# Moving the modulation blocks of a two-layer PEER block into its first expert search, with fewer expert columns ahead

## The chip, the cores and the metric

One core of one Trainium2 chip runs the whole program. The metric is device microseconds (us) for one execution. Engines are called TensorE (PE in the profile; PEld is its weight load), VectorE (DVE), ScalarE (ACT), GpSimd (POOL) and SyncE (SP, the queue from which nearly all transfers are issued, in order).

## The reference, cut to what matters

512 tokens of width 1024 pass through two blocks. Each has a token mixer (gated linear attention in the first, retention and stick-breaking attention in the second) and then PEER, a feed-forward layer with 16384 single-neuron experts: eight heads pick 16 experts each per token by product keys.

```python
def peer(h, w_query, sub_keys, expert_down, expert_up):
    ...
    top_s, top_i = lax.top_k(sub_scores, K)
    ...
    best_s, best_c = lax.top_k(cand_s.reshape(T, PEER_HEADS, K * K), K)
    ...
        act = jax.nn.gelu(a, approximate=False) * gb
        v = expert_up[ib]
        return jnp.einsum('pe,ped->pd', act.astype(xb.dtype), v)
```

The second block is modulated: `mod = silu(c) @ ada_w + ada_b` gives six rows of 1024 values, which scale, shift and gate the second block. They depend on `c` alone, so they can be made at any time before the second block starts.

## The kernel before, in words

A float32 product is made of three matmuls (high times high, low times high, high times low), for which every weight is split: ScalarE copies it to a high part (`uH`, `VH`, `WH`), VectorE subtracts that from the original (`uL`, `VL`, `WL`).

Each of the two PEER layers runs in two parts, one after the other on the same engines.

*The search.* `top_k` makes the query product (`qy`), the key scores (`sc`) and VectorE's top 16 of them, in 16 steps. Then `pick` combines candidates, and for three of the four token tiles a one-hot product writes a dense table of gates to DRAM: 32 steps per tile, each with two comparisons on VectorE (`oh`, `og`, L1022 and L1025) and eight small matmuls (`pg`, L1042). Into all this the search weaves matmuls of the dense product of tokens with the experts' inputs, `pu` (L908, class `Inward`), as filler: `PICK_MM` per step of `pick`, `QUAD_MM` per step of the first two tiles, `LAST_MM` per step of the third. 24 of these matmuls make the activations of 128 experts, `A`; two such columns are a group, and there are 64 groups. `NEARLY` of them are made ahead in the search, and their `A` goes to DRAM (`ad`, L981). The cap on the filler is `NEARLY * 48 + 144`.

*The loop.* It runs over the 64 groups p. Each takes 36 matmuls of 512 columns into `acc` (L119 to L121), for which VectorE makes `W = A * G` (L1102), two `WL` and two `VL` (L1088). Groups not made ahead are made here: where group p+2 is such a group, 48 `pu` matmuls are woven into p. `load_a(p + LA)` at the start of p loads the `A` that went to DRAM; `A` has 12 buffers. The first token tile's experts are not dense: their rows are gathered by GpSimd's indirect transfers (L864) into `gr` and used by VectorE as dot products (L876) and sums (L883). The fetches not made in the search (190 of 256) are spread over the loop by a weight per group, 4 for a group with `pu` matmuls and 1 for one without, up to the sixth group from the end.

*The modulation.* 48 blocks of 128 outputs are each a transfer of 512 KB (`aw`) and a row-wise product with `silu(c)`, summed. 22 are made before the first mixer. The other 26 were split: `side(step, pool)`, called once per step of the first `top_k` (steps -16 to -1) and once per second group of the first loop (steps 0 to 16), took one block per step. In the search GpSimd multiplies (L1689) and ScalarE sums (L1685); in the loop VectorE does both in one instruction (L1177). Step 15 adds the bias, step 16 writes the result to DRAM and reads two rows back.

*The seams.* Between the layers, small row-wise operations stand alone: `hg = h * gf` (L1736, GpSimd for three of four tiles), `h + sh` (L1745, GpSimd for one), `xn + shift` (L199, GpSimd for three), `h + m` (L1797, GpSimd for half), and the last additions (L1833, GpSimd for three halves). The other instances run on VectorE.

Of the kernel before, what the change touches and what calls it, by code (L numbers as in the profile page):

```python
# [17 lines left out]
ALU = mybir.AluOpType  # L18
# [5 lines left out]
NT = 4  # L24
# [8 lines left out]
JUMPS = (16, 8, 5, 4, 3, 2, 2, 2)  # L33
SUBE = lambda nc: nc.vector
GRP = 2
NEARLY = 44
NHELD = 0
FRONT = 4
MLAG = 1
# [9 lines left out]
MT = 16  # L49
FW = 4  # L50
WB = (0, 2)
LA = 2
AB = FRONT + 2
HGP = (0, 1, 2)
ADA = (8, 7, 7)
ADA0 = 0
SHB = (0,)
HALVES = ((0, 512), (512, 1024))
S1 = 2
YR = 2  # L60
# [14 lines left out]
M2_LAG = 4  # L75
SB = 1
SPE = 0
SHP = 3
RP_ACT = (0, 1)
PICK_MM = 40  # L80
QUAD_MM = 20
LAST_MM = 16
PK = 2
LAG = 3
DOT = (2, 2, 1)
# [7 lines left out]
class K:  # L93
# [83 lines left out]
    def rms_rows(self, pool, t, row, gain, out=None, shift=None, known=None):  # L177

        nc = self.nc
        rs = pool.tile([128, 1], F32, name=f"rs{t}", tag="rrs", bufs=NT)
        j = pool.tile([128, D], F32, name="rsj", tag="rsj", bufs=1)
        o = 512 if known is not None else 0
        self.square_mean(rs, j[:, o:], row[:, o:])
        yield
        if known is None:
            nc.vector.tensor_scalar(rs, rs, EPS, None, op0=ALU.add)
        else:
            nc.vector.scalar_tensor_tensor(rs, rs, EPS, known, op0=ALU.add, op1=ALU.add)  # L190
        nc.gpsimd.tensor_tensor(rs, rs, self.mhalf, op=ALU.pow)
        if out is None:
            out = pool.tile([128, D], F32, name=f"xn{t}", tag="xn", bufs=NT)
        yield
        for c in HALVES:
            c = slice(*c)
            nc.vector.scalar_tensor_tensor(out[:, c], row[:, c], rs, gain[:, c], op0=ALU.mult, op1=ALU.mult)
            if shift is not None:
                (nc.gpsimd if t < SHP else nc.vector).tensor_tensor(out[:, c], out[:, c], shift[:, c], op=ALU.add)  # L199
        yield  # L200
        self.turn(out, t)

# [972 lines left out]
def ada_block(K_, b, raw, cs, mod):  # L1175

    K_.nc.vector.scalar_tensor_tensor(raw, raw, 1.0, cs, op0=ALU.mult, op1=ALU.mult, accum_out=mod[:, b:b + 1])  # L1177
# [363 lines left out]
def body(tc, a, out, stop=None):  # L1541
    nc = tc.nc
    with ExitStack() as ctx:
        k = K(ctx, tc, a)
        c = k.const
# [5 lines left out]
        mod = c.tile([128, 48], F32, name="mod")  # L1551
# [127 lines left out]
        def side(step, pool):  # L1679

            if step == -15:
                nc.scalar.activation(cs, cs, AF.Silu)
            while summing:
                b, raw = summing.pop(0)
                nc.scalar.activation(raw, raw, AF.Copy, accum_out=mod[:, b:b + 1])  # L1685
            while loaded:
                b, raw = loaded.pop(0)
                if step < 0:
                    nc.gpsimd.tensor_tensor(raw, raw, cs, op=ALU.mult)  # L1689
                    summing.append((b, raw))  # L1690
                else:
                    ada_block(k, b, raw, cs, mod)
            if left and step >= -15 and step != -2 and step != -1:
                raw = wide(pool, 6) if step < 0 else wide(pool)
                nc.sync.dma_start(raw, a["ada_w"][left[0]])
                loaded.append((left.pop(0), raw))
            if step == MT - 1:
                nc.vector.tensor_tensor(mod, mod, ab, op=ALU.add)
                for i in range(2):
                    s = mod[:, 24 * i + 8:24 * i + 16]  # L1700
                    nc.vector.tensor_scalar(s, s, 1.0, None, op0=ALU.add)
                    nc.vector.tensor_tensor(s, s, ng[:, i], op=ALU.mult)
            if step == MT:
                p = k.mm_tile("mt", tag="u")
                nc.tensor.transpose(p[:48, :128], mod, k.ident)
                m = wide(pool)
                nc.scalar.activation(m[:48, :128], p[:48, :128], AF.Copy)
                nc.sync.dma_start(modd, m[:48, :128])
                row(cs, 1)
                sh.append(row(wide(pool), 0))  # L1710

        class Between:
# [14 lines left out]
            def rows(self, t, parts):  # L1727
                h, n = self.h[t], D // len(parts)
                for i, p in enumerate(parts):
                    s = h[:, i * n:(i + 1) * n]  # L1730
                    nc.vector.tensor_tensor(s, s, p, op=ALU.add)
                yield
                v = ada.tile([128, 2], F32, name="v", tag="v", bufs=NT)
                k.square_mean(v[:, 0:1], self.junk, h)
                hg = self.tile("wide")
                (nc.gpsimd if t in HGP else nc.vector).tensor_tensor(hg, h, gf, op=ALU.mult)  # L1736
                yield
                k.square_mean(v[:, 1:2], self.junk, hg)
                yield
                nc.vector.tensor_scalar(v[:, 0:1], v[:, 0:1], EPS, None, op0=ALU.add)  # L1740
                nc.vector.scalar_tensor_tensor(v[:, 1:2], v[:, 0:1], EPS, v[:, 1:2], op0=ALU.mult, op1=ALU.add)
                nc.gpsimd.tensor_tensor(v, v, k.mhalf.to_broadcast([128, 2]), op=ALU.pow)
                yield
                nc.vector.scalar_tensor_tensor(h, hg, v[:, 1:2], cs, op0=ALU.mult, op1=ALU.mult)
                (nc.gpsimd if t in SHB else nc.vector).tensor_tensor(h, h, sh[0], op=ALU.add)  # L1745
                yield
                if t == 0:
                    yield
                k.turn(h, t)
                self.out.append((t, hg, v))  # L1750
# [18 lines left out]
        with ExitStack() as c1:  # L1769
            mp = pool_of(c1, "mp2")  # L1770
            MH = mp.tile([128, NK, T], F32R, name="MH")
            ML = mp.tile([128, NK, T], F32R, name="ML")
            cos, sin = mp.tile([128, T], F32, name="cos"), mp.tile([128, T], F32, name="sin")
            rv = [mp.tile([128, 512], F32, name=f"rv{t}") for t in range(NT)]
            for t, p in end.first:
                by = lambda x: x.rearrange("p (h d) -> p h d", h=8)
                nc.vector.tensor_tensor(by(rv[t]), by(p), grow[:, t, :, None].to_broadcast([128, 8, 64]), op=ALU.mult)
            ms.close()
            with ExitStack() as c3:
                pool = pool_of(c3, "mx2")  # L1780
                prod = Product(k, ws, 28, MH, ML, OUT_ORDER)
                mixer2(k, c3, pool, rv, cos, sin, MH, ML, ws, prod)
            ms.enter_context(tc.manual_schedule())
            pool = pool_of(c1, "po2")
            h = [pool.tile([128, D], F32, name=f"h{t}") for t in range(NT)]
            hn = pool_of(c2, "gt2", side="right").tile([128, D], F32, name="ghn")
            for t in range(NT):
                nc.sync.dma_start(h[t], x2[t])
            g1, shift, scale = (row(pool.tile([128, D], F32, name=f"row{i}"), i) for i in (2, 3, 4))
            steps = Steps()  # L1790

            def add(half):
                def f(t, p):
                    c_ = slice(half * 512, (half + 1) * 512)
                    m = pool.tile([128, 512], F32, name="m", tag="m", bufs=2)
                    nc.vector.tensor_tensor(m, p, g1[:, c_], op=ALU.mult)
                    (nc.vector if half else nc.gpsimd).tensor_tensor(h[t][:, c_], h[t][:, c_], m, op=ALU.add)  # L1797
                    if half:
                        steps.add(k.rms_rows(pool, t, h[t], scale, hn if t == 0 else None, shift, k.half_mean(pool, t, h[t][:, :512])))
                        steps.step()  # L1800
                return f

            for _ in prod.parts([3]):
                pass
            for t in range(NT):
                add(0)(t, prod.outs[t])
            ws.ready(33)
            ah = Ahead(k, a["peer_w_query_2"], a["peer_sub_keys_2"], a["peer_down_2"], 4)
            token_rows(k, ws, 32, MH, ML, ["acc", "acc", "mm", "mm"], add(1), tail=True, order=OUT_ORDER)
            first = by_halves(k, ah.ws, steps)  # L1810
            for t in range(NT):
                nc.sync.dma_start(x3[t], h[t])

        class Last:
# [10 lines left out]
            def rows(self, t, parts):  # L1825
# [4 lines left out]
                yield  # L1830
                for i in range(2):
                    s = slice(i * 512, (i + 1) * 512)
                    (nc.vector if t == NT - 1 or i else nc.gpsimd).tensor_tensor(y[:, s], y[:, s], self.h[t][:, s], op=ALU.add)  # L1833
                    nc.sync.dma_start(out[t * 128:(t + 1) * 128, s], y[:, s])

            def close(self, steps):
# [109 lines left out]
```

## Time and profile before

| what | value |
|---|---|
| median of three runs | 3200.78 us (3193.4 to 3206.52) |
| the profiled execution, its own time | 3198.14 us |
| its span in the trace | 3196.4 us |
| TensorE, VectorE, ScalarE, GpSimd busy | 97%, 80%, 42%, 31% of the span |
| granted TensorE clock, mean | 0.987 |
| transfers | 819 MB, mean 256 GB/s |

The profiled execution is 2.64 us below the median. Busy time of TensorE counts matmuls that overlap, so the share alone doesn't tell the pace; durations of stretches with known numbers of matmuls do. An idle time behind a row names what ended it.

### The profile page before, as it was taken

To read this page: it belongs to the slowest core of one execution; us is meant where nothing else is said; L and a number is where in the kernel's file an instruction comes from. 1 tells how busy PE (TensorE), PEld (TensorE's weight loads), DVE (VectorE), ACT (ScalarE), POOL (GpSimd) and SP (SyncE) were. 2 spreads that over 40 slices of the span, in tenths; PEclk is the share of its full clock that TensorE was granted. 3 is DMA by queue.
4 is the path that set the end of the run, shared out by engine and by line. 5 is a ranking of instruction groups with operands and counts; after the bars stand their busy time and mean duration, and the time that the engine had idled before them with its cause. 6 is when DMAs were issued, how large, how long until landed. Compare 5 with 4: busy or idle time off the path is not lost.

```text
span 3196.4 us, 45048 instructions
## 1 busy us (share of the span) xinstructions
PE 3085.1 (97%) x16481; PEld 2681.8 (84%) x16481; DVE 2559.8 (80%) x4759; ACT 1350.6 (42%) x1913; POOL 990.7 (31%) x780
## 2 busy tenths in 40 slices
PE   7999999999999999999999999999999999999998
PEld 5777789999988777887777777899999888888876
DVE  6776788888968888888766858888889688888886
ACT  3543334655643333333344642246556433333322
POOL 0442221222414444444212321012224154444441
PEclk9999999999999999999999999999999999999999
DMA  7113346888999999989832132368889999999896
GB/s 277 66 60 126 132 147 210 275 284 287 370 326 356 358 363 345 343 330 342 300 104 86 50 119 88 109 210 274 286 284 369 320 357 357 352 344 352 334 339 224
DMA packets 340735, 819.23 MB, mean 256 GB/s; under 512 B 29920, under 2 KB 173728, under 8 KB 340256
## 3 DMA queue, kind: packets, MB, share of 16 engines
q1 hardware_dynamic: 264016, 544.84, 48.3%
q0 software_dynamic: 73728, 268.47, 22.7%
q10 hardware_dynamic: 2768, 3.04, 0.3%
q8 instruction: 129, 2.11, 0.3%
q14 instruction: 94, 0.77, 0.1%
HBM read 720.79 MB, written 93.35 MB: 255 GB/s over the span
## 4 chain that ended last, share of the span: by engine, by line
PE 54%; issue 17%; DVE 14%; POOL 9%; ACT 3%; DMA 3%; POOLq 0%; SPq 0%; ACTq 0%; DVEq 0%
PE pu L908 26%; POOL gr L864 8%; PE pc L328 5%; PE pg L1042 3%; DVE gacc L883 3%; DVE VL L1088 2%; PE qy L121 2%; PE tr L120 2%; PE tr L121 2%; PE qy L120 2%; PE tr L119 2%; PE acc L120 2%; PE acc L121 2%; PE acc L119 2%; DVE uL L264 2%
## 5 line engine op out<-in xcount | busy, mean ns | idle before, releaser
L908 PE MATMUL pu<-XH,uL 128*128 128x384 f32 x2048 | 697.1, 340 | 9.2 <-DVE uL L264 8.9
L908 PE MATMUL pu<-XH,uH 128*128 128x384 f32 x2048 | 696.7, 340 | 2.1 <-ACT uH L254 2.1
L908 PE MATMUL pu<-XL,uH 128*128 128x384 f32 x2048 | 696.1, 340 | 0.0
L119 PE MATMUL acc<-VH,WH 128*128 128x512 f32 x1536 | 608.7, 396 | 28.2 <-ACT WH L1082 18.8
L120 PE MATMUL acc<-VL,WH 128*128 128x512 f32 x1536 | 604.9, 394 | 12.0 <-DVE VL L1088 11.8
L121 PE MATMUL acc<-VH,WL 128*128 128x512 f32 x1536 | 607.2, 395 | 0.0
L264 DVE TENSOR_TENSOR uL<-sr,uH 128x1024 fp32r<-128x1024 f32 x360 | 449.8, 1253 | 162.7 <-ACT uH L254 159.3
L254 ACT ACTIVATE uH<-sr 128x1024 fp32r<-128x1024 f32 x360 | 378.9, 1054 | 135.8 <-PE tr L121 81.9
L1082 ACT ACTIVATE WH<-W 128x384 fp32r<-128x384 f32 x256 | 134.3, 524 | 706.2 <-DVE W L1102 706.1
L908 PEld LDWEIGHTS pu<-XH,uL 128*128 128x128 f32 x2048 | 386.0, 188 | 16.0 <-DVE uL L264 11.7
L908 PEld LDWEIGHTS pu<-XH,uH 128*128 128x128 f32 x2048 | 386.0, 188 | 6.5 <-ACT uH L254 2.8
L908 PEld LDWEIGHTS pu<-XL,uH 128*128 128x128 f32 x2048 | 386.2, 189 | 4.2
L119 PEld LDWEIGHTS acc<-VH,WH 128*128 128x128 f32 x1536 | 291.1, 189 | 101.2 <-ACT WH L1082 36.9
L864 POOL DMA_INDIRECT gr<-in_peer_down_rows_dram,gid x128 | 198.3, 1549 | 571.8 <-DVE gr L876 394.4
L1088 DVE TENSOR_TENSOR VL<-vr,VH 128x1024 fp32r<-128x1024 f32 x256 | 315.1, 1231 | 55.8 <-ACT VH L1082 55.0
L864 POOL DMA_INDIRECT gr<-in_peer_u_rows_dram,gid x128 | 198.0, 1547 | 502.0 <-DVE gr L876 408.3
L121 PEld LDWEIGHTS acc<-VH,WL 128*128 128x128 f32 x1536 | 291.1, 190 | 71.4 <-DVE WL L1088 11.7
L120 PEld LDWEIGHTS acc<-VL,WH 128*128 128x128 f32 x1536 | 291.3, 190 | 71.1 <-DVE VL L1088 18.1
L883 DVE SCALAR_TENSOR_TENSOR gacc<-gr,ga,gacc 128x1024 f32<-128x1024 f32 x254 | 325.9, 1283 | 1.8
L915 ACT ACTIVATE A<-pu 128x384 f32<-128x384 f32 x256 | 127.0, 496 | 470.8 <-PE pu L908 466.7
L876 DVE SCALAR_TENSOR_TENSOR gr<-gr,ghn 128x1024 f32<-128x1024 f32 x256 | 310.4, 1218 | 0.0
L1088 DVE TENSOR_TENSOR WL<-W,WH 128x384 fp32r<-128x384 f32 x256 | 143.0, 559 | 160.5 <-ACT WH L1082 159.9
(402 smaller groups left out, 4840.1 us busy)
## 6 DMA issues: line engine op xcount, KB each, us to landing
sr<-in_peer_u_dram SPq DMA_DIRECT2D x128, 512.0 KB
vr<-in_peer_v_dram SPq DMA_DIRECT2D x128, 512.0 KB
sr<-in_peer_down_dram SPq DMA_DIRECT2D x128, 512.0 KB
vr<-in_peer_up_dram SPq DMA_DIRECT2D x128, 512.0 KB
gd<-st SPq DMA_DIRECT2D x96, 512.0 KB
G<-gd SPq DMA_DIRECT2D x64, 768.0 KB
ad<-A SPq DMA_DIRECT2D x176, 192.0 KB
A<-ad SPq DMA_DIRECT2D x176, 192.0 KB
```

Of the source, the lines that this page charges most:

```text
L119: mm(out, lH, rH, start=start, stop=False)
L120: mm(out, lH, rL, start=False, stop=False)
L121: mm(out, lL, rH, start=False, stop=stop)
L254: nc.scalar.activation(H, raw, AF.Copy)
L264: self.K_.nc.vector.tensor_tensor(L, raw, H.bitcast(F32), op=ALU.subtract)
L328: K_.nc.tensor.matmul(p, w[:, s], x[:, k, :], start=k == 0 and i == 0, stop=k == NK - 1 and i == 2)
L864: self.K_.nc.gpsimd.indirect_dma_start(out=r, out_offset=None, in_=self.V if v else self.U, in_offset=bass.IndirectOffsetOnAxis(ap=self.id ...
L876: nc.vector.scalar_tensor_tensor(r, r, 1.0, self.hn, op0=ALU.mult, op1=ALU.mult, accum_out=w)
L883: nc.vector.scalar_tensor_tensor(self.acc, r, w, self.acc, op0=ALU.mult, op1=ALU.add)
L908: nc.tensor.matmul(self.p[:, :TD], w, x, start=i == 0, stop=i == 23)
L1082: nc.scalar.activation(part[0], src, AF.Copy)
L1088: nc.vector.tensor_tensor(L, src, H.bitcast(F32), op=ALU.subtract)
```

## The change

Three things are changed together. All 26 late modulation blocks are loaded in steps -15 to -3 of the first search, two per step, and all are multiplied on GpSimd and summed on ScalarE; the loop has none. `NEARLY` goes from 44 to 40, with the filler counts 40, 20, 16 down to 36, 18, 15, and `load_a` runs three groups ahead in place of two. All row-wise operations of the seams run on VectorE.

```diff
-NEARLY = 44
+NEARLY = 40
...
-LA = 2
+LA = 3
...
-PICK_MM = 40
-QUAD_MM = 20
-LAST_MM = 16
+PICK_MM = 36
+QUAD_MM = 18
+LAST_MM = 15
...
-                (nc.gpsimd if t < SHP else nc.vector).tensor_tensor(out[:, c], out[:, c], shift[:, c], op=ALU.add)
+                nc.vector.tensor_tensor(out[:, c], out[:, c], shift[:, c], op=ALU.add)
...
                 b, raw = loaded.pop(0)
-                if step < 0:
-                    nc.gpsimd.tensor_tensor(raw, raw, cs, op=ALU.mult)
-                    summing.append((b, raw))
-                else:
-                    ada_block(k, b, raw, cs, mod)
-            if left and step >= -15 and step != -2 and step != -1:
-                raw = wide(pool, 6) if step < 0 else wide(pool)
-                nc.sync.dma_start(raw, a["ada_w"][left[0]])
-                loaded.append((left.pop(0), raw))
+                nc.gpsimd.tensor_tensor(raw, raw, cs, op=ALU.mult)
+                summing.append((b, raw))
+            if -15 <= step < -2:
+                for b in left[:2]:
+                    raw = wide(pool, 6)
+                    nc.sync.dma_start(raw, a["ada_w"][b])
+                    loaded.append((left.pop(0), raw))
...
-                (nc.gpsimd if t in HGP else nc.vector).tensor_tensor(hg, h, gf, op=ALU.mult)
+                nc.vector.tensor_tensor(hg, h, gf, op=ALU.mult)
...
-                (nc.gpsimd if t in SHB else nc.vector).tensor_tensor(h, h, sh[0], op=ALU.add)
+                nc.vector.tensor_tensor(h, h, sh[0], op=ALU.add)
...
-                    (nc.vector if half else nc.gpsimd).tensor_tensor(h[t][:, c_], h[t][:, c_], m, op=ALU.add)
+                    nc.vector.tensor_tensor(h[t][:, c_], h[t][:, c_], m, op=ALU.add)
...
-                    (nc.vector if t == NT - 1 or i else nc.gpsimd).tensor_tensor(y[:, s], y[:, s], self.h[t][:, s], op=ALU.add)
+                    nc.vector.tensor_tensor(y[:, s], y[:, s], self.h[t][:, s], op=ALU.add)
```

## Rows read from the trace of the kernel before

**Rows 1.** The page's head and its first part: busy time, share, instructions.

```profile
span 3196.4 us, 45048 instructions
...
PE   3085.1 (97%) x16481; PEld 2681.8 (84%) x16481; DVE 2559.8 (80%) x4759; ACT 1350.6 (42%) x1913; POOL 990.7 (31%) x780
```

**Rows 2.** Stages as windows: stretch, its length, each engine's busy time (instructions), clock, DMA.

```profile
core 0: us, PE busy (x) PEld busy (x) DVE busy (x) ACT busy (x) POOL busy (x), PEclk, DMA share, GB/s
344.80:447.00 102.20, 98.08 (x491) 81.39 (x490) 94.78 (x494) 40.19 (x60) 36.93 (x31) 1.00 0.42 158
447.00:531.10 84.10, 80.31 (x452) 79.64 (x452) 67.39 (x241) 31.45 (x45) 5.57 (x5) 0.98 0.54 176
531.10:656.70 125.60, 125.60 (x873) 121.01 (x872) 110.72 (x217) 71.93 (x88) 23.96 (x15) 1.00 0.83 276
...
784.90:888.30 103.40, 103.40 (x750) 98.93 (x748) 99.78 (x145) 63.56 (x73) 47.97 (x32) 1.00 1.01 356
...
928.00:1468.00 540.00, 524.15 (x2393) 438.54 (x2392) 448.73 (x574) 182.90 (x251) 231.51 (x159) 1.00 0.92 343
...
1949.50:2046.40 96.90, 96.90 (x491) 81.57 (x490) 87.25 (x494) 24.33 (x32) 1.09 (x18) 1.00 0.28 98
...
2528.40:3046.00 517.60, 514.84 (x2391) 439.92 (x2391) 432.97 (x543) 182.48 (x250) 229.45 (x159) 1.00 0.92 342
```

**Rows 3.** The chain that ended last, one filler step of the first search.

```profile
544.18 3.54 PE pu L908 x20
```

**Rows 4.** Windows of the loops: three plain groups, one with filler, three near the end.

```profile
2602.90:2627.40 24.50, 24.50 (x110) 20.29 (x109) 19.45 (x29) 10.11 (x14) 9.76 (x7) 1.00 1.02 397
2586.30:2602.90 16.60, 16.60 (x85) 15.20 (x84) 15.41 (x25) 4.54 (x7) 10.69 (x7) 1.00 0.92 334
1484.00:1517.60 33.60, 28.68 (x109) 21.80 (x108) 28.79 (x32) 9.24 (x13) 14.94 (x12) 0.90 0.93 344
```

**Rows 5.** Waits in the first loop, 928 to 1468 us: total, times, longest.

```profile
PEld acc L119 <- ACT WH L1082: 20.6, 23, 1.9
...
DVE W L1102 <- DMA A<-ad: 8.8, 3, 4.2
```

**Rows 6.** The same wait in the second loop, 2528.4 to 3046 us.

```profile
PEld acc L119 <- ACT WH L1082: 7.0, 10, 0.9
```

**Rows 7.** L1177's window in the first loop: VectorE's modulation blocks, two instructions each.

```profile
928.00:1468.00 540.00, 15.93 (x26) 1.00 0.92 343
```

**Rows 8.** Groups by line in the first `top_k`: total, mean ns, idle before.

```profile
L1689 POOL TENSOR_TENSOR aw<-aw,cs 128x1024 f32<-128x1024 f32 x13 | 35.9, 2766 | 74.9 <-DMA aw<-in_ada_w_dram 74.9
L264 DVE TENSOR_TENSOR uL<-sr,uH 128x1024 fp32r<-128x1024 f32 x14 | 24.6, 1756 | 0.0
```

**Rows 9.** The same VectorE line in the second `top_k`, which has no modulation.

```profile
L264 DVE TENSOR_TENSOR uL<-sr,uH 128x1024 fp32r<-128x1024 f32 x14 | 16.9, 1205 | 0.0
```

**Rows 10.** Timeline of the first `top_k`, GpSimd's products beside VectorE's subtractions: start, duration.

```profile
354.03 4.72 POOL L1689 TENSOR_TENSOR aw<-aw,cs 128x1024 f32<-128x1024 f32 x2 [27.72 <-DMA aw<-in_ada_w_dram]
357.12 2.71 DVE L264 TENSOR_TENSOR uL<-sr,uH 128x1024 fp32r<-128x1024 f32 x1
385.33 3.53 POOL L1689 TENSOR_TENSOR aw<-aw,cs 128x1024 f32<-128x1024 f32 x1 [2.94 <-DMA aw<-in_ada_w_dram]
385.39 1.21 DVE L264 TENSOR_TENSOR uL<-sr,uH 128x1024 fp32r<-128x1024 f32 x1
398.38 3.36 DVE L264 TENSOR_TENSOR uL<-sr,uH 128x1024 fp32r<-128x1024 f32 x1
```

**Rows 11.** Groups by line: a sum row of the gather, and the seams' GpSimd operations.

```profile
L883 DVE SCALAR_TENSOR_TENSOR gacc<-gr,ga,gacc 128x1024 f32<-128x1024 f32 x254 | 325.9, 1283 | 1.8
L1736 POOL TENSOR_TENSOR vr<-gr,gf 128x1024 f32<-128x1024 f32 x3 | 7.4, 2475 | 43.2 <-DVE gr L1731 43.2
L1797 POOL TENSOR_TENSOR h<-h,m 128x512 f32<-128x512 f32 x4 | 6.0, 1533 | 16.5 <-DVE m L1796 16.5
L199 POOL TENSOR_TENSOR xn<-xn,row 128x512 f32<-128x512 f32 x4 | 5.6, 1415 | 0.0
```

**Rows 12.** Timeline of the seam after the first loop: subtractions beside GpSimd's products.

```profile
1591.42 3.41 DVE L1088 TENSOR_TENSOR VL<-vr,VH 128x1024 fp32r<-128x1024 f32 x1
1600.27 3.41 DVE L264 TENSOR_TENSOR uL<-sr,uH 128x1024 fp32r<-128x1024 f32 x1
```

**Rows 13.** SyncE's queue after step 16 of the modulation.

```profile
1311.82 0.34 SPq L1565 DMA_DIRECT2D cs<-modd  x1
...
1312.87 1.28 SPq L1071 DMA_DIRECT2D A<-ad  x2
```

More of the change, by code (lines that the diff above doesn't have):

```diff
@@ L51 @@
 WB = (0, 2)
-LA = 2
+LA = 3
 AB = FRONT + 2
-HGP = (0, 1, 2)
 ADA = (8, 7, 7)
 ADA0 = 0
-SHB = (0,)
 HALVES = ((0, 512), (512, 1024))
@@ L77 @@
 SPE = 0
-SHP = 3
 RP_ACT = (0, 1)
-PICK_MM = 40
-QUAD_MM = 20
-LAST_MM = 16
+PICK_MM = 36
+QUAD_MM = 18
+LAST_MM = 15
 PK = 2
```

## The prediction, made before the change was run

> **What bounds the kernel now.** I read the page first: TensorE is busy for 97% of the span and VectorE comes second [rows 1]. Busy time alone can't say where TensorE loses time, so the next view is the windows by stage, for both layers, which run the same code [rows 2]. The reader is to compare equal stages. The first loop's 49 groups up to the last filler take 540.0 us, the second's 517.6 us with as many matmuls (x2393 and x2391). The first `top_k` takes 102.2 us, the second 96.9 us, again with equal matmuls. Both differences lie where the first layer has modulation blocks. In the searches' one-hot part (531.1 to 656.7 us) TensorE is busy throughout and VectorE for 88% of the time; in the third tile's part (784.9 to 888.3 us) VectorE reaches 96%.
>
> Then the pace of TensorE. One filler step of 20 `pu` matmuls takes 3.54 us, 0.177 us each [rows 3]. Three plain groups of the loop take 24.5 us, 8.17 us each; a group with 48 filler matmuls takes 16.6 us, so filler costs (16.6 - 8.17) / 48 = 0.176 us there too [rows 4]. Filler costs the same in either place: moving it gains only where another engine holds TensorE back. The floor of a loop's 49 groups is 49 x 8.17 + 13 x 48 x 0.176 = 510 us. The first loop loses 30 us over it, the second 7.5 us. The waits say to what: weight loads of `acc` wait for the high part of `W`, which comes from VectorE's multiplication, 20.6 us in the first loop [rows 5] and 7.0 us in the second [rows 6]; and VectorE waits 8.8 us for `A` from DRAM in the first [rows 5].
>
> **Filler moves from search to loop.** The search made 24 + 11 x 40 + 64 x 20 + 32 x 16 = 2256 filler matmuls (11 yields of `pick`), exactly the old cap. It will make 24 + 11 x 36 + 64 x 18 + 32 x 15 = 2052, under the new cap of 2064. So 204 go to each loop, at 0.177 us: 36 us added there per layer. At most 36 us come off each search, but only while TensorE bounds it. `pick` could give 44 x 0.177 = 7.8 us; TensorE is idle for 3.8 us of its 84.1 us already [rows 2], and I take 6.5. The first two tiles could give 64 x 0.177 = 11.3 us each. VectorE's 110.7 us lose 64 / 24 = 2.7 subtractions of 1.2 us [rows 9], leaving 107.4 us under a new TensorE time of 114.3 us: TensorE stays the bound, and I take 10.5 each for steps that are uneven. The third tile could give 5.7, to 97.7 us, but VectorE's 99.8 us lose only 1.6 us, to 98.2; with its transfers already at a share of 1.01 [rows 2] I take 3.5. Together 31 us, with 24 and 36 as ends. Cost of the move: 5 us per layer, 10 in all (0 to 24).
>
> **The first loop without modulation.** 13 instructions of 1.22 us leave VectorE, 15.9 us [rows 7], and 13 transfers of 512 KB leave SyncE's queue. Nothing else differs in kind between the two loops, except step 16, whose read of `modd` stood in SyncE's queue before the `A` loads [rows 13]; it stays, and loading three groups ahead gives those loads 8.17 us more. Loads of `vr` and `gr` behind `load_a` meet no new wait: with the new order of late groups at most 11 of the 12 `A` buffers are live. Besides, VectorE's load per group falls: 190 gathered rows are spread by weights whose sum was 15 x 4 + 43 = 103 and will be 19 x 4 + 39 = 115, so a group with filler gets 6.6 rows in place of 7.4, at 1.28 us each [rows 11], 1 us less of the 15.4 us that VectorE works in its 16.6 us [rows 4]. I take 4.5 us of loss for the first loop in place of 30, a gain of 25 (14 to 29), and 4 for the second, a gain of 3.5 (0 to 7).
>
> **The loops' ends.** Filler runs out before heavy gathers do. At 1484.0 us three groups take 33.6 us where plain ones take 24.5 [rows 4], 9 us of VectorE's gathers. The new order has filler to group 51 and a quarter of it at 54, and heavy gathers without filler only at 57 (54 and 57 for 51 and 55 before), with 0.8 rows fewer each. I take 2 us per loop, 4 in all (0 to 8).
>
> **The first `top_k`.** GpSimd gets 26 products in place of 13, at 2.77 us 72 us of work in 102.2 [rows 8]. The 13 now there made VectorE's 14 subtractions 24.6 us in place of 16.9 [rows 9]: where GpSimd starts first, the subtraction takes 2.7 to 3.4 us; where they start together it may take 1.2 and GpSimd is drawn out to 3.5 [rows 10]. That cost 102.2 - 96.9 = 5.3 us [rows 2]. With pairs, two products of 2.4 us would just fit between two subtractions (6.5 us per step less 1.2), because the loads are issued behind a load that waits for the subtraction. So the cost need not double: I take 3 us more. From below, -3, if the second product pushes all collisions off; from above, every one of 13 steps stalls by 3.36 - 1.21 = 2.1 us [rows 9, 10], less the 0.6 us per step that VectorE has spare ((96.9 - 87.25) / 16, [rows 2]): 20 us, 14 more than now. ScalarE's 13 more sums (16 us) fit beside its 40 us of 102.2 [rows 2]; they stand before the next `uH`, whose subtraction waits for VectorE's scores anyway. Without that cover each would add 1.2 us per step. SyncE's 13 more issues stand behind no new wait: their six buffers are free a step before.
>
> The Trainium skill, page "SBUF — State Buffer", section "Who interferes with whom", speaks against this part: a VectorE instruction with two SBUF inputs and a GpSimd instruction that reads SBUF exclude each other for the whole instruction, whoever comes first. By that, the upper end above would be the sum, +14 in place of +3.
>
> **The seams.** VectorE takes three products of `hg` (2.48 us on GpSimd), four halves of `h + m` (1.53 us) and four of `xn + shift` (1.42 us) [rows 11], plus one `h + sh` and three last halves. On VectorE a full row costs about 1.2 us, half of that a half row. That lengthens its queue ahead of `VL` and `uL`, for which TensorE waits. Against it: GpSimd's operations stretched a `VL` and a `uL` there to 3.41 us each [rows 12], over 2 us too long. Net I take a gain of 2 us (6 gained to 4 lost).
>
> **Sum.** +10 (move) - 25 - 3.5 (loops) - 4 (ends) + 3 (`top_k`) - 2 (seams) = -21.5 us, from the profiled execution's 3198.14 us to 3176.6; it stood 2.64 us under the median of the runs shown, so 3179 us against 3200.78.
>
> **Rivals.** *GpSimd locks VectorE out.* Every pair meets a subtraction: 11 us more than forecast, 3190 us. For it: 2.7 and 3.4 us [rows 10]. Against: the phase set by the loads. It decides once more than about 5 of 13 steps stall.
> *The surplus stays.* The first loop's 30 us are due to transfers (a share of 0.92 in both loops [rows 2]) and to step 16, not to VectorE: half stays, 13 us more, 3192 us. For it: the waits for `A` [rows 5]. Against: the second loop has the same share.
> *The searches do not get shorter* (slower than before). VectorE takes over there and the steps keep their length; the loops still grow by 36 us each: 2 x 31 us more, 3241 us. It decides if VectorE's work per step of the first two tiles exceeds TensorE's new 3.57 us (114.3 / 32); now it is 110.7 / 32 = 3.46 us [rows 2] before it loses 0.1. Half of it would give 3210 us.
> *More than forecast.* The loops reach their floor and the searches give all 36 us: 3158 us.
> That the change doesn't do what it says can be excluded but for the surplus rival: the steps and counts are written out.
>
> **How the numbers follow.** Under 0.5% (16 us) a measurement can't tell a difference. Forecast 0.60, of which 0.10 above 3184.8 us (its terms' errors); lock 0.13; surplus 0.12; searches 0.08; more 0.07. Faster: 0.50 + 0.07 + 0.05 (a mild form of the two middle rivals) = 0.62. Same: 0.10 + 0.20 = 0.30. Slower: 0.08. The range runs from 3158, the best case, to 3202, past both middle rivals with 10 us for their errors, and leaves out the last rival and the tails of the others.
>
> **What would show it.** No L1177 in the first loop and its 49 groups' loss near the second's; the one-hot steps of the first two tiles at 114.3 / 32 = 3.57 us in place of 125.6 / 32 = 3.93; `pu` windows of the search with 204 fewer matmuls; subtractions in the first `top_k` at a mean under 2 us. A mean near 3 us there, one-hot steps over 3.8 us, or `acc` still waiting 15 us for `WH` in the first loop would make it wrong.

## The result and the profile after

The changed kernel takes 3152.3 us (median of 4; 3148.9 to 3154.1) against 3198.6 us (median of 4: the three executions shown before the change and one more): a ratio of 0.9852, 95% interval 0.9829 to 0.9875, 46 us faster. The forecast was 21.5 us faster, and its range ended at 3158: the gain was forecast too small, and the time lies outside the range by 6 us. The page of the changed kernel, beside [rows 1]:

```profile
span 3147.2 us, 44959 instructions
...
PE 3061.4 (97%) x16481; PEld 2682.9 (85%) x16481; DVE 2543.1 (81%) x4750; ACT 1367.5 (43%) x1939; POOL 965.8 (31%) x776
```

The shares don't tell where 49 us of span went. The windows by stage do; they answer to [rows 2], here in order: first `top_k`, `pick`, the three tiles, the way to the loop, the first loop's 49 groups, its groups 49 to 60, its last three, the seam and second mixer up to the second `top_k`, that `top_k`, then the second loop's 49 groups and its groups 49 to 60.

```profile
core 0: us, PE busy (x) PEld busy (x) DVE busy (x) ACT busy (x) POOL busy (x), PEclk, DMA share, GB/s
347.40:450.40 103.00, 98.39 (x492) 81.35 (x490) 96.38 (x494) 53.73 (x86) 71.81 (x44) 1.00 0.59 221
450.40:526.90 76.50, 72.73 (x408) 72.06 (x408) 64.74 (x238) 28.54 (x41) 4.88 (x4) 0.98 0.55 173
526.90:641.10 114.20, 114.20 (x808) 109.64 (x807) 106.46 (x213) 69.00 (x82) 21.63 (x17) 1.00 0.88 289
641.10:757.90 116.80, 116.80 (x839) 112.25 (x837) 108.07 (x214) 72.61 (x86) 22.24 (x17) 1.00 0.90 292
757.90:856.20 98.30, 98.08 (x718) 93.00 (x715) 97.20 (x144) 60.45 (x70) 44.97 (x32) 1.00 1.02 364
856.20:894.50 38.30, 37.52 (x234) 36.72 (x235) 18.05 (x21) 19.62 (x27) 2.56 (x2) 1.00 1.00 366
894.50:1431.50 537.00, 537.00 (x2536) 466.30 (x2535) 441.69 (x556) 192.87 (x263) 221.69 (x159) 1.00 0.92 339
1431.50:1546.10 114.60, 111.72 (x494) 92.22 (x493) 93.04 (x106) 38.69 (x53) 42.26 (x30) 0.99 0.89 324
1546.10:1577.10 31.00, 27.68 (x118) 22.25 (x117) 24.24 (x30) 13.78 (x20) 0.73 (x1) 0.94 0.52 183
1577.10:1917.10 340.00, 319.69 (x1590) 254.06 (x1588) 220.40 (x355) 163.75 (x286) 76.81 (x111) 0.97 0.26 85
1917.10:2014.10 97.00, 97.00 (x491) 81.67 (x490) 87.35 (x494) 23.02 (x30) 1.09 (x18) 1.00 0.28 97
2459.30:2994.90 535.60, 535.60 (x2535) 466.79 (x2533) 441.45 (x552) 192.42 (x262) 222.06 (x159) 1.00 0.92 338
2994.90:3109.40 114.50, 111.65 (x494) 92.30 (x494) 93.13 (x107) 38.65 (x53) 42.29 (x30) 0.99 0.89 324
```

For the ends of the loops before, groups 49 to 60 of the first and the second:

```profile
1467.70:1578.90 111.20, 103.62 (x433) 82.09 (x433) 90.89 (x104) 36.17 (x50) 39.23 (x30) 0.97 0.90 334
3045.70:3158.10 112.40, 105.03 (x433) 83.07 (x432) 91.40 (x105) 36.47 (x50) 39.24 (x30) 0.95 0.89 331
```

The reader is to see three things. The first tile's stage falls from 125.6 to 114.2 us, the full 64 x 0.177 = 11.3 us, with TensorE still busy throughout; from the start of `pick` to the loop the first search is 36.9 us shorter, the second 36.8. The loops' middles now have TensorE busy for 537.00 of 537.00 us and 535.60 of 535.60; their floor grows by 144 filler matmuls to 510 + 25.4 = 535.4 us, so the losses of 30 and 7.5 us are now 1.6 and 0.2. And the ends, with 60 more filler matmuls (10.6 us, floor 98.0 + 10.6 = 108.6), lose 6.0 and 5.9 us in place of 13.2 and 14.4.

A part of the ends' loss is the clock. A group that gets the weight of 4 is called heavy here, the others plain. Before the change TensorE was busy for 4.42 us of 7.30 after a heavy group without filler, and for the next 6.8 us its granted clock was 0.50, the level of 1.2 GHz:

```profile
1499.00:1506.30 7.30, 4.42 (x18) 2.77 (x16) 6.25 (x8) 1.47 (x2) 4.19 (x3) 1.00 1.00 387
1506.30:1513.10 6.80, 5.73 (x14) 4.48 (x15) 4.84 (x7) 2.94 (x4) 2.02 (x2) 0.50 0.95 328
```

At half the clock, 6.8 us cost an estimated 3.4 us at most, since TensorE also waited in them. In the second loop's end it was 6.8 and 3.4 us at 0.50, at most 5.1 us. After the change each end has one such stretch of 3.4 us, at most 1.7 us; the first loop's:

```profile
1528.30:1531.70 3.40, 3.40 (x8) 2.26 (x8) 2.42 (x4) 1.47 (x2) 0.00 (x0) 0.50 0.55 170
```

A run further down (`e12_weight6`) has an end without such a stretch, which took 114.4 us, and the other with one of 3.4 us, which took 116.0.

In the first `top_k` GpSimd has twice the work, and the stage is 0.8 us longer:

```profile
L1685 POOL TENSOR_TENSOR aw<-aw,cs 128x1024 f32<-128x1024 f32 x26 | 69.8, 2714 | 46.0 <-DMA aw<-in_ada_w_dram 45.8
L261 DVE TENSOR_TENSOR uL<-sr,uH 128x1024 fp32r<-128x1024 f32 x14 | 26.2, 1874 | 0.0
```

### The profile page after: what moved, and what is told of

It is laid out like the page before. It is cut to its first block, busy times and chain, and to the rows that moved or that the text cites. A ratio compares the mean times of both kernels' runs of the same rounds, so it can differ in the third digit from the quotient of the medians.

```text
span 3147.2 us, 44959 instructions
## 1 busy us (share of the span) xinstructions
PE 3061.4 (97%) x16481; PEld 2682.9 (85%) x16481; DVE 2543.1 (81%) x4750; ACT 1367.5 (43%) x1939; POOL 965.8 (31%) x776
## 4 chain that ended last, share of the span: by engine, by line
PE 41%; DVE 6%; issue 1%; ACT 1%; DMA 1%; POOL 0%; SPq 0%; ACTq 0%; DVEq 0%; POOLq 0%
PE pu L905 14%; PE acc L117 5%; PE acc L118 5%; PE acc L116 5%; PE pc L325 2%; DVE gr L873 1%; DVE uL L261 1%; PE tr L118 1%; PE tr L117 1%; PE tr L116 1%; PE qy L117 1%; PE qy L118 1%; PE qy L116 1%; PE pg L1039 1%; DVE gacc L880 1%
## 5 line engine op out<-in xcount | busy, mean ns | idle before, releaser
L905 PE MATMUL pu<-XH,uH 128*128 128x384 f32 x2048 | 706.0, 345 | 0.0
L116 PE MATMUL acc<-VH,WH 128*128 128x512 f32 x1536 | 601.8, 392 | 4.0 <-ACT VH L1079 3.4
L861 POOL DMA_INDIRECT gr<-in_peer_down_rows_dram,gid x128 | 186.0, 1453 | 557.7 <-DVE gr L873 383.0
L861 POOL DMA_INDIRECT gr<-in_peer_u_rows_dram,gid x128 | 186.2, 1454 | 471.9 <-DVE gr L873 385.7
L1079 ACT ACTIVATE VH<-vr 128x1024 fp32r<-128x1024 f32 x256 | 268.0, 1047 | 11.9 <-PE acc L118 5.3
```

Source lines behind the costliest of these rows:

```text
L116: mm(out, lH, rH, start=start, stop=False)
L861: self.K_.nc.gpsimd.indirect_dma_start(out=r, out_offset=None, in_=self.V if v else self.U, in_offset=bass.IndirectOffsetOnAxis(ap=self.id ...
L905: nc.tensor.matmul(self.p[:, :TD], w, x, start=i == 0, stop=i == 23)
L1079: nc.scalar.activation(part[0], src, AF.Copy)
```

## The experiments

Three kinds of runs: each part alone on the kernel before; single parts taken out of the changed kernel; and one weight or one cost varied. Losses are lengths over the floors above. "Theory one" stands for VectorE's work per group as the cause of the loops' losses, "theory two" for late loads of `A`.

### Each part alone

All 26 blocks in the first search (`e1_blocks`), the hunk of `side` in the diff alone. 

> The kernel before, with all 26 late blocks made in the first search and nothing else changed. Theory one (VectorE's work per group sets the loops' loss): the first loop's 49 groups fall from 540 us to the second loop's 518, the first top_k grows by 1 us as in the changed kernel (102.2 to 103.0), the groups from 49 on and the second layer stay; about 21 us faster. Theory two (late loads of A set it): the loss stays above 15 of 30 us, less than 15 us faster.

40 groups ahead (`e2_forty`):

```diff
-NEARLY = 44
+NEARLY = 40
-PICK_MM = 40
-QUAD_MM = 20
-LAST_MM = 16
+PICK_MM = 36
+QUAD_MM = 18
+LAST_MM = 15
```

> The kernel before, with 40 groups ahead and the filler counts 36, 18, 15 alone. Theory one: each search is 36 us shorter, each loop has 36 us more filler, and the second layer loses nothing in the middle of its loop (8 to 1 us) and half at its end (14.5 to 6): 16 us faster there; the first loop, still with 13 blocks on VectorE, loses about 20 of its 30 us still and gains 7 at its end: 17 us faster; 30 us faster in all (25 to 38). Theory two: the loops' losses stay as they are, at most 5 us faster.

`A` three groups ahead (`e3_three_ahead`):

```diff
-LA = 2
+LA = 3
```

> The kernel before, with A loaded three groups ahead alone. Theory one: only the 8.8 us in which VectorE waits for A in the first loop can go: 0 to 9 us faster, the second loop's 517.6 us unchanged. Theory two: the first loop gains 15 us or more and the second loop's loss goes too, 20 us faster.

The seams on VectorE (`e4_seams`), in effect the `nc.vector` hunks of the diff alone. 

> The kernel before, with every row-wise operation of the seams on VectorE alone. Both theories: between 4 us faster and 2 us slower, since the changed kernel's stretch from the end of the first loop to the second top_k is 340.0 us against 339.7 and its last three groups 31.1 and 31.4 us against 30.9 and 32.2.

Measured, against 3198.1 us: blocks 3184.6 us, ratio 0.996 (0.9948 to 0.9973); forty 3156.8 us, 0.987 (0.9846 to 0.9893); three ahead 3194.0 us, 0.9985 (0.9974 to 0.9996); seams 3201.2 us, 1.0009 (0.9997 to 1.002). The first loop's 49 groups with the blocks gone, with forty alone, and with `A` three ahead alone:

```profile
929.00:1452.90 523.90, 519.19 (x2391) 439.99 (x2390) 433.57 (x548) 182.64 (x250) 230.07 (x159) 1.00 0.92 340
```
```profile
894.80:1442.50 547.70, 543.26 (x2535) 467.35 (x2535) 455.84 (x582) 191.49 (x263) 234.00 (x159) 0.99 0.92 344
```
```profile
928.30:1458.50 530.20, 521.91 (x2390) 438.55 (x2390) 447.99 (x574) 182.78 (x250) 231.27 (x159) 1.00 0.93 350
```

Forty alone brings 41 of the 46 us, more than the 25 to 38 expected. The second loop's 49 groups with forty alone stand on their floor:

```profile
2468.80:3004.30 535.50, 535.50 (x2534) 466.78 (x2533) 441.78 (x550) 192.51 (x262) 222.69 (x159) 1.00 0.91 337
```

In the first loop the loss of 30 falls to 13.9 without the blocks, to 12.3 with forty, to 20 with earlier loads: the three gains add up to 44 where only 30 are to be had, so they overlap. Blocks missed their expectation of 21 us (13.5, under the 15 that was theory two's mark), and late loads are a part of what they leave. Step 16's reads stand ahead of the loads of `A` [rows 13] as group 35 begins. Groups 35 and 36, whose floor is 24.8 us, took, before, without the blocks, and with `A` three ahead:

```profile
1311.10:1342.30 31.20, 27.77 (x121) 22.97 (x120) 23.23 (x26) 9.75 (x13) 11.99 (x8) 0.95 0.89 329
1297.10:1327.60 30.50, 27.80 (x121) 22.96 (x120) 23.24 (x26) 9.76 (x13) 11.99 (x8) 0.94 0.91 330
1306.20:1332.10 25.90, 25.28 (x121) 21.77 (x120) 22.13 (x26) 9.76 (x13) 11.21 (x8) 1.00 1.00 374
```

So theory two holds for some 5 of the 30 us, in which the clock (0.95 and 0.94 in the first two rows) has a share. As the main cause it is out: the second loop's 49 groups take 517.1 us with `A` three ahead (517.6 before), and forty alone clears their loss. The seams are worth nothing that can be told.

### Single parts taken out of the changed kernel

`A` two groups ahead again (`e5_two_ahead`):

```diff
-LA = 3
+LA = 2
```

> The changed kernel with A loaded two groups ahead, as before. By itself the third group ahead gave the first loop 9.5 us. Theory one (rows of the gather per group decide; late loads only matter while VectorE is full): at most 3 us slower than the changed kernel, about 3153 to 3155 us, the loss of the first loop's 49 groups from 3 to at most 6 us. Theory two (late loads of A make the loss): the first loop's loss is back at 10 us or more, 3160 us or more.

The blocks split between search and loop again (`e9_blocks_in_loop`): the `side` hunk reversed. 

> The changed kernel with the late blocks split between the first search and the first loop again. Theory one: with fewer rows per group the first loop has room for most of the 13 blocks (forty groups alone lost 13.8 us there with blocks and A two ahead): a loss of 6 to 11 us in place of 3, so 3 to 8 us slower than the changed kernel; the first top_k stays within 2 us. A rival, that the blocks are the larger part of the gain, as the prediction had it: 15 us slower or more.

Measured: 3150.4 us, ratio 0.9854 (0.9835 to 0.9873), and 3151.1 us, 0.9849 (0.9832 to 0.9866): neither can be told from the changed kernel. For the blocks 3 to 8 us slower had been expected. The first loop's 49 groups, first with two ahead, then with the blocks in it:

```profile
889.60:1428.20 538.60, 537.54 (x2534) 466.01 (x2533) 442.02 (x556) 192.66 (x263) 224.78 (x159) 1.00 0.92 337
```
```profile
895.10:1432.70 537.60, 537.53 (x2535) 465.94 (x2534) 455.72 (x582) 192.31 (x263) 232.43 (x159) 1.00 0.94 351
```

With 13 blocks VectorE is busy 14 us longer (455.72 against 441.69) and the stage takes 0.6 us more. Once forty and the earlier loads are in, the move of the blocks, which I had given the largest term, is worth nothing that can be told. With loads two ahead it is worth something: the stage takes 547.70 us with forty and the blocks in it (forty alone) and 538.60 without them. Of the 12.3 us that forty leaves, either the blocks' move or the third group ahead takes most.

### What forty does: the weights of the gathered rows

A weight of 3 on the kernel before (`e11_weight3`):

```diff
-FW = 4
+FW = 3
```

> The kernel before with a weight of 3 in place of 4 for groups with filler: 190 rows by 15 x 3 + 43 = 88 make 6.5 rows per heavy group (7.4 before, 6.6 in the changed kernel) and 2.2 per plain one; filler, blocks and loads unchanged. Theory one (rows per heavy group decide): the second loop's middle loss falls from 8 to 4 us or less, the first's from 30 to below 22, each end from 14 to about 10: 15 to 20 us faster. Theory two (filler and transfers decide): within 4 us of the kernel before.

Measured: 3179.9 us, ratio 0.9943 (0.9925 to 0.9961), 21 us faster at its median, with no filler, block or load changed. The first loop's middle takes 529.4 us (loss 19.4), the ends 3 to 4 us less each, and the second loop's middle loses 2.7 us:

```profile
2519.70:3032.50 512.80, 511.82 (x2390) 440.45 (x2389) 431.68 (x544) 181.85 (x249) 231.69 (x159) 1.00 0.93 346
```

So the distribution of VectorE's rows sets much of the loss. But the next runs showed that "rows per heavy group" is not the rule.

Heavy rows only where a group has filler of its own, on the changed kernel (`e6_weights`) and, with the same edit, on the kernel before (`e7_weights_before`):

```diff
-    weights = [FW if p + 2 >= FRONT and fresh(p + 2) else 1 for p in range(n - 1)]
+    weights, rest = [], NE * 24 - inw.mm
+    for p in range(n - 1):
+        own = p + 2 >= FRONT and fresh(p + 2) and rest >= 24 * GRP
+        weights.append(FW if own else 1)
+        rest -= 24 * GRP * own
```

> The changed kernel with the heavy share of gathered rows only on groups that still have filler of their own (up to group 51 in place of 57), the same 190 rows in all. Theory one: the 6 us that each loop loses in the groups 58 and 59 go, and heavy groups get 6.97 rows in place of 6.61, which they still hold: 9 to 12 us faster than the changed kernel, 3140 to 3143 us. Theory two: the ends are held by the last transfers and stay, within 3 us of the changed kernel.

Measured: 3139.7 us, ratio 0.9817 (0.9798 to 0.9835), the fastest kernel of the study. Its first loop's middle stays at 536.90 us with 7.0 rows per heavy group, and its end, groups 49 to 60, stands on the floor, so the last transfers don't hold it (theory two):

```profile
1433.10:1541.70 108.60, 108.60 (x494) 91.66 (x493) 82.81 (x98) 39.04 (x53) 29.57 (x22) 1.00 0.83 298
```

The timeline of VectorE in a plain group of the second loop before, which took 8.9 us, gave the next theory:

```profile
2816.96 0.55 DVE L1102 TENSOR_TENSOR W<-A,G 128x384 f32<-128x384 f32 x1
2818.10 0.56 DVE L1088 TENSOR_TENSOR WL<-W,WH 128x384 fp32r<-128x384 f32 x1 [0.59 <-ACT WH L1082]
2819.05 1.23 DVE L1088 TENSOR_TENSOR VL<-vr,VH 128x1024 fp32r<-128x1024 f32 x1 [0.39 <-ACT VH L1082]
2820.19 1.28 DVE L883 SCALAR_TENSOR_TENSOR gacc<-gr,ga,gacc 128x1024 f32<-128x1024 f32 x1
2821.39 0.55 DVE L1102 TENSOR_TENSOR W<-A,G 128x384 f32<-128x384 f32 x1
```

Each half of a group is a chain: `W`, 0.59 us of waiting for ScalarE's `WH`, `WL`, 0.39 us for `VH`, `VL`, and one gathered row. From `W` to `W` it takes 4.43 us, 8.86 per group with two rows, against TensorE's 8.17. In such a group VectorE sets the pace while it is busy for only 6.93 of 8.90 us:

```profile
2817.00:2825.90 8.90, 8.63 (x38) 6.62 (x37) 6.93 (x10) 2.95 (x4) 2.02 (x2) 1.00 0.98 357
```

The some 7 us that the second loop's middle lost before lie in ten groups, each 0.5 to 0.9 us over the floor; eight of them are plain.

Balance theory: what plain groups fall behind must be made good in the next heavy group, where TensorE takes 16.6 us. Before, there were 2.75 plain groups with 1.84 rows to a heavy one with 7.4; with forty there are 2 with 1.65 to one with 6.6. Two runs were made to test it.

> The kernel before with the heavy share of rows only on groups that have filler of their own (up to group 48 in place of 55): 190 rows by 13 x 4 + 45 = 97 make 7.8 rows per heavy group and 1.96 per plain one. Balance theory (in a plain group VectorE's chain with two rows takes 8.86 us, since it also waits twice for ScalarE, against TensorE's 8.17; what plain groups fall behind, heavy ones must make good): the ends' losses of 13 and 14.5 us go to 1 or less, the middle of the second loop loses more, 12 to 16 us in place of 8; 10 to 18 us faster in all. Rival (the ends are held by the last transfers): ends unchanged.

Measured: 3186.8 us, ratio 0.995 (0.993 to 0.9969). Ends 100.0 us each (loss 2.0, with 1 or less expected), so the rival that the last transfers hold them is out. Both middles got worse, as the balance has it, by some 4 and 3 us; but the second's loss is 10.7 us where 12 to 16 were expected, and the middles now also hold ten rows that came from the ends, so more rows per plain group are not told apart from more rows in all. The second loop's middle and end:

```profile
2530.90:3051.60 520.70, 516.07 (x2390) 438.53 (x2389) 443.53 (x553) 182.75 (x249) 249.79 (x169) 1.00 0.94 349
3051.60:3151.60 100.00, 99.60 (x433) 80.02 (x432) 79.14 (x94) 36.20 (x50) 25.96 (x20) 1.00 0.86 321
```

A weight of 6 on the changed kernel (`e12_weight6`):

```diff
-FW = 4
+FW = 6
```

> The changed kernel with a weight of 6 in place of 4: 190 rows by 19 x 6 + 39 = 153 make 7.5 rows per heavy group, as many as before the change (7.4), and 1.2 per plain one. Theory one in its first form (rows per heavy group decide): the middles of both loops lose 8 us or more each, as the second loop did before; 20 us slower than the changed kernel. Balance theory: a plain group with 1.2 rows needs less than 8.17 us, so the middles stay within 2 us, and only the ends, where heavy groups have no filler, lose 2 to 4 us more each: 4 to 8 us slower.

Measured: 3154.7 us, ratio 0.9852 (0.9834 to 0.9869). With 7.5 rows per heavy group, as before the change, the second middle stays on its floor:

```profile
2465.00:3000.60 535.60, 535.60 (x2535) 466.95 (x2534) 442.56 (x550) 192.62 (x262) 224.78 (x158) 1.00 0.92 338
```

That rules out the first form of theory one. The balance theory missed the ends, which lost at most 1.5 us more in place of 2 to 4, and as a plain sum it misses the weight of 3 too: a heavy group and its 2.75 plain ones hold 12.4 rows there as they did before, yet the second middle's loss fell from 7.5 to 2.7 us. How VectorE's lead is built up and used is not settled.

### Where the search turns, and GpSimd's price

The fastest kernel with 36 groups ahead (`e13_36`):

```diff
-NEARLY = 40
+NEARLY = 36
-PICK_MM = 36
-QUAD_MM = 18
-LAST_MM = 15
+PICK_MM = 32
+QUAD_MM = 16
+LAST_MM = 14
```

> The best kernel so far (the changed kernel with heavy rows only on groups with filler) with 36 groups ahead and filler counts 32, 16, 14: 204 matmuls more move from each search to each loop. The loops have nothing left to gain and grow by 36 us each. If VectorE takes over the searches now (106 of 114 us in the first tiles before this step, 97 of 98 in the third): they give back 22 to 30 us of 36, and the kernel is 12 to 28 us slower than 3139.7. If TensorE still bounds them: within 4 us of it.

Measured: 3165.0 us, ratio 0.9888 (0.987 to 0.9905), 25 us slower than with 40. Up to group 60 each loop grows by 36 us, on its floor; the searches give back some 25 us each; the first tile's stage gives back only 8.0 of 11.3 us, the third's 1.2 of 5.7. In the first tile's stage TensorE is no longer busy throughout, and filler waits for VectorE's subtractions, a wait that the changed kernel doesn't have there:

```profile
520.60:626.80 106.20, 103.98 (x749) 98.73 (x748) 102.33 (x210) 65.28 (x78) 26.28 (x19) 1.00 0.90 294
```
```profile
PE pu L905 <- DVE uL L261: 2.2, 2, 1.2
```

So the rival of searches that don't get shorter comes in one step further on, in part: about 25 of 36 us still come back.

The changed kernel without GpSimd's products (`e8_no_product`); the modulation is left out:

```diff
-                nc.gpsimd.tensor_tensor(raw, raw, cs, op=ALU.mult)
```

> The changed kernel without GpSimd's products in the first search: the sums are taken of the raw weights, so the modulation is left out. If GpSimd's products are what makes the first top_k longer than the second: 97 to 98 us in place of 103.0, and no subtraction there over 1.5 us. If it is the 26 transfers and ScalarE's sums: 101 us or more.

Measured, in one execution: the first `top_k` takes 97.0 us, exactly the second's, with all 26 transfers and sums in place; all 14 subtractions are back at 1.2 us:

```profile
343.10:440.10 97.00, 97.00 (x491) 81.69 (x490) 87.36 (x494) 53.69 (x86) 1.08 (x18) 1.00 0.64 238
L261 DVE TENSOR_TENSOR uL<-sr,uH 128x1024 fp32r<-128x1024 f32 x14 | 16.9, 1204 | 0.0
```

GpSimd's 26 products cost 6.0 us; 13 cost 5.3 by the difference of the two layers before. These two can't be told apart: the stage took 102.2 to 105.0 us in the seven profiles with 13 products and 103.0 to 105.4 in the six with 26.

## Why the prediction was wrong, by its own steps

**Direction** held, and with it that VectorE's work held TensorE back in the loops, that filler costs the same in either place and that TensorE bounds the searches. All the signs that were named came true: losses of 1.6 and 0.2 us in the two loops, one-hot steps of the first tile at 3.57 us, subtractions at a mean of 1.87 us, no wait of `acc` for `WH` left in the first loop. They test the direction and not the size. What failed is which part of the change frees the loops: the move of filler was booked as a cost of 10 us and the blocks' move as the main gain; alone, the move of filler brings 41 us and the blocks 13.5. The sum was too small by 28 us in the span's terms (49.2 against 21.5): 12 from the move, 12 from the ends, 7 from the middles and 2 from `top_k`, less 2 from the seams and 2.6 from the stretch ahead of the first `top_k`.

**"Cost of the move: 5 us per layer"** failed. I discounted the search for uneven steps, a busy VectorE and transfers; 36.9 and 36.8 us came off in place of 31, as much as the loops' floors grew. The first two tiles gave 11.4 us each in place of 10.5, the third 5.1 in place of 3.5, though VectorE is busy there for 97.20 of 98.30 us, and `pick` 7.6 in place of 6.5. The upper end of 36 was right: 12 us of the error. That VectorE's limit lay just behind is shown by the 36-group run.

**"I take 2 us per loop" for the ends** failed, and its bound of 8 us for both as well: 7.2 and 8.5 us. I priced the heavy rows one by one. Each of the two heavy groups without filler, 51 and 55, was followed by lost time before (9.1 us in groups 52 and 53, 3.7 in 56 and 57 of the first loop); after, 51 has filler, 54 with 12 filler matmuls and 6.6 rows costs nothing, and only 57 is left, with 5.9 us in groups 58 and 59. With heavy rows kept to groups with filler nothing is lost. That a pile of rows costs time once it exceeds VectorE's lead fits this, and is argued. The clock was left out as well: [rows 4] shows 0.90 in the stretch of which 9 us were read as gathers, so up to an estimated 3.4 us of them are clock, and of the 7.2 and 8.5 us up to 1.7 and 3.4 are clock that came back. 12 us of the error, and the reason why the range's lower end missed: it took the ends at 4 us. (By its own terms that best case comes to about 3161 us, not 3158.)

**The loops' middles** were sized as 25 and 3.5 us and measured 28 and 7.3, 7 us of the error. That the first loop's 25 came near is in part luck, for its attribution failed: I gave most of the surplus to the 13 blocks, and fewer rows per group a small share. The blocks alone bring 16 us there, forty alone 18, and with forty and earlier loads in, the blocks cost 0.6. VectorE's busy share of 83% looks like room; a plain group with two rows is bound by a chain in which VectorE waits for ScalarE. The Trainium skill, page "Perfetto Trace Analysis", section "Identifying the Most-Contended Engine", calls occupancy a fair measure, for VectorE, of how close one is to the roofline. Here it doesn't tell which engine holds the group: VectorE set the pace while busy for 6.93 of 8.90 us.

**The first `top_k`** was right in kind: 3 us forecast, 0.8 measured, which is within the spread of the profiles, and the run without products shows that the products are all of its surplus. The Trainium skill's page "SBUF — State Buffer", section "Who interferes with whom", holds here in that a blocked subtraction waits out GpSimd's product (2.95 to 3.1 us in place of 1.2); the sum worked out from it, +14 us, did not come. Pairs leave every second subtraction alone: five of the 14 took 2.95 us or more, a sixth 1.47, the others 1.2. **The seams** (2 us forecast) gave nothing: 340.0 us against 339.7 from the loop's end to the second `top_k`. The remaining 2.6 us is the stretch ahead of the first `top_k`, which the change doesn't touch and which lay between 342 and 349 us in all profiles. The rivals: the lock didn't happen; the surplus rival's mechanism was there (groups 35 and 36), but the third group ahead, a part of the change, took it away; "more than forecast" did happen, and was given 0.07.

Open: forty adds filler to the loops, sets the heavy groups closer and gives each fewer rows. The weights were varied and the count of groups ahead, but not the spacing of heavy groups by itself, nor the filler at the same weights and spacing. So that forty brings the gain is shown; by which of these, the weight runs tell only in part.

## What to carry to other kernels

Before pricing a move of filler, find for each stage whether TensorE's pace or a chain of another engine sets its length, and read that chain from one group's timeline, waits for a third engine included; here an engine busy for 78% of a group set its pace. Spread an engine's side work by the time that the bounding engine leaves in each group, and stop where that filler ends: this one edit gave 12.6 us on top of the change. On the kernel before, the same edit gave back 24 us at the ends and took 7 in the middles, so the groups must have room for what is moved into them. Read the clock of a stretch before all of its loss is laid to a wait. Run each part of a bundled change alone: here one of three brought nearly all, and the others overlapped with it.

## What was unexpected of the hardware

Twice the GpSimd products cost VectorE's 14 subtractions 26.2 us in place of 24.6 and the stage no more than can be told. The changed kernel's timeline of the first `top_k` shows how: one step is hit (2.98 us), and by the next subtraction (1.20 us) the second product of the pair is done and the next pair not yet begun.

```profile
372.22 5.74 POOL L1685 TENSOR_TENSOR aw<-aw,cs 128x1024 f32<-128x1024 f32 x2 [0.16 <-DMA aw<-in_ada_w_dram]
372.72 2.98 DVE L261 TENSOR_TENSOR uL<-sr,uH 128x1024 fp32r<-128x1024 f32 x1
380.37 1.20 DVE L261 TENSOR_TENSOR uL<-sr,uH 128x1024 fp32r<-128x1024 f32 x1
380.88 5.30 POOL L1685 TENSOR_TENSOR aw<-aw,cs 128x1024 f32<-128x1024 f32 x2 [2.92 <-DMA aw<-in_ada_w_dram]
```

And VectorE kept up in the third tile's stage at 97.20 of 98.30 us busy, with transfers at a share of 1.02.
